# Hymba layer: gates of three second halves in pieces, meta rows in 34 columns, activation tiles by group

## The chip, the cores and the metric

The kernel runs on one core of a Trainium2 chip. Its engines are TensorE (PE, with its weight loads PEld), VectorE (DVE), ScalarE (ACT), GpSimd (POOL) and SyncE (SP), which issues the transfers. Each engine takes its instructions in a fixed order; a wait of one instruction holds all that stand behind it on the same engine. The metric is the device time of one launch in microseconds, as a median over runs.

## The reference

One decoder layer: 16 meta tokens are put ahead of 1024 tokens, a projection of 1024 to 3584 features feeds four heads of differential attention and four heads of HGRN2, an output projection follows, and a feed-forward part with a causal convolution of width 3 between its 1024 to 5632 and 2816 to 1024 products. The meta tokens are dropped at the end. In the feed-forward part the gate half of the 5632 features goes through the convolution and gelu and is multiplied with the up half. All in float32.

```python
def reference(x, meta_tokens, rel_bias_table, hgrn_lb_logits, ln_mix_pre, ln_mix_post,
              w_in, diff_lambda, diff_subln, hgrn_gnorm, w_out, ln_ffn_pre, ln_ffn_post,
              w_ffn_up, ffn_conv_w, ffn_conv_b, w_ffn_down):
...
    h = jnp.concatenate([meta, x], axis=1)
...
        a = rmsnorm(h, ln_mix_pre[l])
        proj = a @ w_in[l]
        dq, dk, dv, hq, hf, hi, hg = jnp.split(proj, SPLITS, axis=-1)
...
        y_diff = diff_attention(dq, dk, dv, diff_lambda[l], diff_subln[l], rel_bias_table, lam_init)
        y_hgrn = hgrn2(hq, hf, hi, hg, lb_all[l], hgrn_gnorm[l])
        mix = jnp.concatenate([y_diff, y_hgrn], axis=-1) @ w_out[l]
        h = h + rmsnorm(mix, ln_mix_post[l])
        a = rmsnorm(h, ln_ffn_pre[l])
        y = conv_ffn(a, w_ffn_up[l], ffn_conv_w[l], ffn_conv_b[l], w_ffn_down[l])
        h = h + rmsnorm(y, ln_ffn_post[l])
    return h[:, N_META:, :]

def conv_ffn(a, w_up, conv_w, conv_b, w_down):
    u = a @ w_up
    u = lax.conv_general_dilated(
...
        feature_group_count=C) + conv_b
    gate, up = jnp.split(u, 2, axis=-1)
    return (jax.nn.gelu(gate, approximate=True) * up) @ w_down
```

## The kernel before

**Numbers.** Every float32 operand of a product is split into a high part and a rest (hi, lo), and a product is three matmuls: hi by hi, hi by lo, lo by hi. Weights are split on ACT (hi) and on DVE or POOL (lo).

**Tokens.** 1040 tokens stand in nine blocks: block 0 are the 16 meta tokens, 1 to 8 have 128 tokens each. GROUPS puts blocks 0 to 2, 3 to 5 and 6 to 8 together: 272, 384 and 384 tokens. The projection (`proj_group`, `proj_step`, lines 219 to 239) goes over a group for each feature tile of 128: eight blocks k of the contraction, three matmuls each, with `ahi` and `alo` (the normalised activations, one tile each of 8 x 1040 floats a partition) as the streamed operand. `pre_hi` and `pre_lo` (lines 275 to 279) fill them from the transposed input.

**Output projection.** It has two halves of 512 columns. `out_first` does the first half while HGRN's last head still runs, with seven of the eight k blocks; the result goes to y0, and the eighth follows in `out_last` as soon as the head is there. Only the last two meta tokens are needed later (the convolution reaches two tokens back), so block 0 has two rows: `m0` holds hi and lo of 2 rows, `out_meta` (line 977) does three matmuls of 2 x 512 for each k through `out_part` (lines 966 to 975). Each `py` and `pz` takes a bank of PSUM by the name ip, of which there are two, so the third tile in line waits until the first has been read. In the second half the loop over blocks (order 1, 2, 0, 3 to 8) takes block 0 through the same `out_part` in four pieces of two k, and `post_a` (post norm and residual) follows each block. The blocks' split operands come back from DRAM as `mp` tiles.

**Feed-forward, up.** The 5632 features are 22 tiles ft of 128 gate and 128 up features. Tiles 0 and 1 are plain products (`plain_unit`). Tiles 2 to 21 are done in `unit` (lines 1322 to 1365): seven products j = 0 to 6 of half size for each half p of the tokens, in place of eight. A product is 12 matmuls of 256 or 258 columns. PE goes j by j and, within j, over p = 0, 1. Products 0 and 4 go to bank pa, 1, 3 and 5 to pb, 2 and 6 to pc. DVE combines them: `u2` behind j=1, `u3` and a part of `uu` behind j=3, the rest of `uu` behind j=5, a part of `ug` behind j=6; ACT copies pa. A bank is written again by PE only after such a combination has read it: j=3 of half p needs `u2` of that half done.

**The gate.** `gated` (line 1288) does the convolution of `ug` (gate) and `uu` (up): for each side ACT makes a shifted and scaled copy c (`conv`, line 1278) and DVE adds two taps to it (SCALAR_TENSOR_TENSOR, c0 for gate and c1 for up); ACT does gelu, POOL multiplies, SP stores to `gsc`. Four taps of 128 x 512 a half, eight a tile.

**Weights.** `prep(q)` makes the split weight q = 7 ft + j one tile ahead: POOL sums raw tiles `ra` to `ws`, ACT rounds to `uh`, DVE or POOL takes the rest to `ul`. It is called at the start of each j of the tile before.

**What sets the order.** The order within an engine comes out of the order of the code, of priorities and of waits that a scheduler plans; `behind(name)` holds instructions back behind a marked one (`u2`, `u3`, `x1`, `shift`). In tile 2 of before, the gate of tile 1's second half, which waits in `waiting`, is done behind `u3`, with four preps; all other gates follow their own half at once.

## Time and profile before

| | us |
|---|---|
| median of 3 runs (1326.83 to 1329.81) | 1327.34 |
| the profiled execution | 1325.77 |
| its span | 1324.0 |
| input projection, attention, HGRN (0 to 530) | 530 |
| output projection, first half (530 to 593) | 63 |
| output projection, second half (593 to 652) | 59 |
| up, plain tiles 0 and 1 (652 to 701) | 49 |
| up, tiles 2 to 21 (701 to 1104) | 403 |
| down (1104 to 1324) | 220 |

The profile's page gives busy time by engine over the whole span. The stages are read from the timeline, and a window of a stage gives the busy time of each engine in it. A row of the timeline has its start, its length, engine, line, operation and operands; in brackets stands how long the engine was idle ahead of it, and what ended that. A row with xN stands for N such instructions in a run.

### The profile page before, as it was taken

What the parts mean: (1) busy time and instruction counts of PE and PEld (TensorE: products, weight loads), DVE (VectorE), ACT (ScalarE), POOL (GpSimd) and SP (SyncE); (2) the same over time, 40 slices, a digit from 0 to 9 for tenths busy, and PEclk for the clock granted to TensorE, in tenths of its full rate; (3) what the DMA queues carried; (4) which work ended last, traced back from release to release, by engine and by line L of the source; (5) the groups of instructions that cost most, each with busy time, mean ns of one, the idle gap of its engine ahead of it and who ended that gap; (6) DMA issues with size and microseconds to landing.
All of it is one profiled execution on the core that took longest, in us unless ns stands there. A gap on an engine that the chain in (4) does not pass through costs nothing.

```text
span 1324.0 us, 26317 instructions
## 1 busy us (share of the span) xinstructions
PE 1276.6 (96%) x10227; PEld 1181.8 (89%) x10227; DVE 912.8 (69%) x1589; ACT 689.4 (52%) x1670; POOL 413.5 (31%) x324
## 2 busy tenths in 40 slices
PE   6999999999999999999999799999999999999997
PEld 5898899989999999777899799999999998888886
DVE  7666557564756465834778777877787876697587
ACT  7465346535654565545665454554454454554454
POOL 3211211121202120112147567667667641010021
PEclk9999999999999999999999899999999999999999
DMA  6331323132311011835713222222222324964363
GB/s 217 109 127 61 101 94 132 56 129 77 124 44 35 33 33 46 262 114 182 242 41 112 84 84 76 92 80 82 81 89 76 105 85 166 343 222 156 107 207 120
DMA packets 84371, 153.07 MB, mean 116 GB/s; under 512 B 9571, under 2 KB 19843, under 8 KB 84246
## 3 DMA queue, kind: packets, MB, share of 16 engines
q1 hardware_dynamic: 84246, 151.39, 34.0%
q8 instruction: 80, 1.31, 0.4%
q14 instruction: 45, 0.37, 0.1%
HBM read 112.69 MB, written 38.67 MB: 114 GB/s over the span
## 4 chain that ended last, share of the span: by engine, by line
PE 71%; DVE 6%; DMA 3%; ACT 3%; issue 2%; POOL 1%; SPq 1%; DVEq 0%; ACTq 0%; POOLq 0%
PE pd L1534 5%; PE pd L1535 5%; PE pd L1533 5%; PE pb L1336 4%; PE pb L1337 4%; PE pb L1338 4%; PE pa L1337 2%; PE pa L1336 2%; PE pa L1338 2%; PE pa L709 2%; PE pc L1338 2%; PE pc L1337 2%; PE pc L1336 2%; PE py L970 2%; PE py L974 2%
## 5 line engine op out<-in xcount | busy, mean ns | idle before, releaser
L1336 PE MATMUL pb<-t,uh 128*128 128x258 f32 (+1 forms) x480 | 135.4, 282 | 10.7 <-DVE u L54 10.7
L1337 PE MATMUL pb<-t,uh 128*128 128x258 f32 (+1 forms) x480 | 135.1, 281 | 0.0
L1338 PE MATMUL pb<-t,ul 128*128 128x258 f32 (+1 forms) x480 | 134.9, 281 | 0.0
L1534 PE MATMUL pd<-wl,gh 128*128 128x512 f32 (+1 forms) x314 | 121.4, 386 | 0.5 <-DVE wl L54 0.5
L1535 PE MATMUL pd<-wh,gl 128*128 128x512 f32 (+1 forms) x314 | 120.6, 384 | 0.0
L1533 PE MATMUL pd<-wh,gh 128*128 128x512 f32 (+1 forms) x314 | 120.1, 383 | 0.0
L54 DVE SCALAR_TENSOR_TENSOR c<-uu,cwt,c 128x512 f32<-128x512 f32 x88 | 92.4, 1050 | 22.5 <-ACT c L54 21.9
L1291 POOL TENSOR_TENSOR c<-c,c 128x512 f32<-128x512 f32 x44 | 68.4, 1554 | 124.1 <-ACT c L54 118.1
L1336 PEld LDWEIGHTS pb<-t,uh 128*128 128x128 f32 x480 | 91.5, 191 | 11.3 <-DVE u L54 11.3
L1337 PEld LDWEIGHTS pb<-t,uh 128*128 128x128 f32 x480 | 91.6, 191 | 0.0
L1338 PEld LDWEIGHTS pb<-t,ul 128*128 128x128 f32 x480 | 91.4, 190 | 0.0
L1337 PE MATMUL pa<-t,uh 128*128 128x258 f32 (+1 forms) x320 | 89.8, 281 | 0.0
L1338 PE MATMUL pa<-t,ul 128*128 128x258 f32 (+1 forms) x320 | 89.7, 280 | 0.0
L1336 PE MATMUL pa<-t,uh 128*128 128x258 f32 (+1 forms) x320 | 89.7, 280 | 0.0
L54 DVE SCALAR_TENSOR_TENSOR c<-ug,cwt,c 128x512 f32<-128x512 f32 x88 | 87.6, 996 | 1.7 <-ACT c L54 1.1
L1338 PE MATMUL pc<-t,ul 128*128 128x256 f32 x320 | 88.3, 276 | 0.0
L1336 PE MATMUL pc<-t,uh 128*128 128x256 f32 x320 | 88.3, 276 | 0.0
L1337 PE MATMUL pc<-t,uh 128*128 128x256 f32 x320 | 88.3, 276 | 0.0
L1534 PEld LDWEIGHTS pd<-wl,gh 128*128 128x128 f32 x314 | 59.0, 188 | 13.6 <-DVE wl L54 1.6
L1533 PEld LDWEIGHTS pd<-wh,gh 128*128 128x128 f32 x314 | 58.9, 188 | 12.6
L1535 PEld LDWEIGHTS pd<-wh,gl 128*128 128x128 f32 x314 | 59.0, 188 | 11.5
L54 ACT ACTIVATE pb<-S,ast 128x528 f32<-128x528 f32 (+7 forms) x72 | 46.5, 647 | 39.1 <-DVE ast L54 38.9
(411 smaller groups left out, 4210.3 us busy)
## 6 DMA issues: line engine op xcount, KB each, us to landing
ra<-in_wup_dram SPq DMA_DIRECT2D x80, 256.0 KB, 2.7
wd<-in_wdown_dram SPq DMA_DIRECT2D x44, 256.0 KB, 4.2
tsc<-wd SPq DMA_DIRECT2D x44, 256.0 KB, 2.7
gsc<-c SPq DMA_DIRECT2D x44, 256.0 KB, 2.0
wi<-tsc SPq DMA_DIRECT2D x44, 256.0 KB, 2.8
gi<-gsc SPq DMA_DIRECT2D x33, 256.0 KB, 3.7
wi<-in_wdown_dram SPq DMA_DIRECT2D x33, 256.0 KB, 3.0
msc<-mm SPq DMA_DIRECT2D x21, 256.0 KB, 3.5
```

The source lines that it names most:

```text
L54: ins = call(*args, **kw)
L709: T.matmul(po[:, :P], w_, vn[:, j], start=(j == 0), stop=(j == i))
L970: T.matmul(py[:r], mh[:, j, :r], hi, start=(first and j == 0), stop=False)
L974: T.matmul(py[:r], ml[:, j, :r], hi, start=False, stop=(last and k == k1 - 1))
L1291: G.tensor_tensor(cg, cg, cu, op=ALU.mult)
L1336: T.matmul(pt, hi[:, s], th[:, k], start=(first and k == 0), stop=False, skip_group_check=True)
L1337: T.matmul(pt, hi[:, s], tl[:, k], start=False, stop=False, skip_group_check=True)
L1338: T.matmul(pt, lo[:, s], th[:, k], start=False, stop=(k == 3), skip_group_check=True)
L1533: T.matmul(py, gh[:, s], wh, start=(k == 0 and pr not in (3, 7)), stop=False, skip_group_check=True)
L1534: T.matmul(py, gh[:, s], wl, start=False, stop=False, skip_group_check=True)
L1535: T.matmul(py, gl[:, s], wh, start=False, stop=(k == NH - 1), skip_group_check=True)
```

## The change

Three parts.

- The activation tiles `ahi` and `alo` become three tiles each, one for each group of blocks, with 272, 384 and 384 floats for each k. 32 floats of padding go ahead of them and 32 into the pool behind. What is computed and in which order stays.
- The two meta rows lie in a tile of 36 columns, hi in columns 0 and 1, lo in 32 and 33, zeros between. `out_meta` multiplies the 34 columns with the weights' hi and then lo: two matmuls for each k. Rows 0 and 1 and rows 32 and 33 of the result are then added: in the first half by an ACT copy and a DVE add into y0, in the second by an ACT copy to `low` and a DVE add in PSUM. The lo by lo product is now in the sum as well. `out_last` and block 1 stay as they were.
- The gates of the second halves (p = 1) of tiles 1, 2 and 3 wait for the next tile, and are done there in pieces: ACT's shifts at j=1 behind `u2` and `x1`, the taps of the up side behind `u3` of half 0, those of the gate side, gelu, product and store after j=3. Preps that would stand at j = 1 and 3 (in tile 2 at all of j = 0 to 3) come behind these pieces. From tile 4 on each gate follows its half at once.

```diff
@@ -180,5 +180,13 @@
     at_cm, atp = pool("at", 1)
-    ahi = atp.tile([P, KD, L], F32R, tag="ahi", name="ahi")
-    alo = atp.tile([P, KD, L], F32R, tag="alo", name="alo")
+    line_up(atp, 32)
+    acts = [[atp.tile([P, KD, start(b1 - 1) + P - start(b0)], F32R, tag=f"a{l}{g}", name=f"a{l}{g}") for g, (b0, b1) in enumerate(GROUPS)]
+            for l in ("hi", "lo")]
+
+    def act(l, ks, t0, t1):
+        g = 0 if t1 <= start(3) else 1 if t1 <= start(6) else 2
+        base = start(GROUPS[g][0])
+        return acts[l][g][:, ks, t0 - base:t1 - base]
+
     ws_cm, wsp = pool("wdsums", 5)
+    wsp.tile([P, 32], F32, tag="lineup_ws", name="lineup_ws", bufs=1)
 
@@ -231,7 +239,7 @@
         s = slice(P * (k % 4), P * (k % 4 + 1))
-        T.matmul(pt, hi[:, s], ahi[:, k, t0:t1], start=(k == 0), stop=False)
+        T.matmul(pt, hi[:, s], act(0, k, t0, t1), start=(k == 0), stop=False)
         yield cost
-        T.matmul(pt, hi[:, s], alo[:, k, t0:t1], start=False, stop=False)
+        T.matmul(pt, hi[:, s], act(1, k, t0, t1), start=False, stop=False)
         yield cost
-        T.matmul(pt, lo[:, s], ahi[:, k, t0:t1], start=False, stop=(k == KD - 1))
+        T.matmul(pt, lo[:, s], act(0, k, t0, t1), start=False, stop=(k == KD - 1))
         if k == KD - 1:
@@ -275,6 +283,6 @@
     def pre_hi(pv, ks, s):
-        return A.copy(ahi[:, ks, s], pv)
+        return A.copy(act(0, ks, s.start, s.stop), pv)
 
     def pre_lo(pv, ks, s):
-        return V.tensor_tensor(alo[:, ks, s], pv, ahi[:, ks, s].bitcast(F32), op=ALU.subtract)
+        return V.tensor_tensor(act(1, ks, s.start, s.stop), pv, act(0, ks, s.start, s.stop).bitcast(F32), op=ALU.subtract)
 
@@ -910,3 +918,4 @@
     y0 = yp.tile([P, NBLK, 512], F32, tag="y0", name="y0")
-    m0 = yp.tile([P, 2, KD, 2], F32R, tag="m0", name="m0")
+    m0 = yp.tile([P, KD, 36], F32R, tag="m0", name="m0")
+    G.memset(m0.bitcast(F32), 0.0)
     ssy = yp.tile([P, NBLK, 4], F32, tag="ssy", name="ssy")
@@ -947,4 +956,3 @@
         if i < 2:
-            m = (m0, kept)[i]
-            hi, lo = m[:, 0, k0:k1], m[:, 1, k0:k1]
+            hi, lo = (kept[:, 0, k0:k1], kept[:, 1, k0:k1]) if i else (m0[:, k0:k1, 0:2], m0[:, k0:k1, 32:34])
         elif k1 - k0 == 1:
@@ -976,4 +984,7 @@
 
-    def out_meta(py, wo, nk):
-        return out_part((m0[:, 0], m0[:, 1], 0, nk, 2), py, wo, True, True)
+    def out_meta(py, wo, k0, k1, last):
+        for k in range(k0, k1):
+            for l in range(2):
+                T.matmul(py[:34], m0[:, k, :34], wo[k][l], start=(k == 0 and l == 0), stop=(k == last and l == 1))
+                yield 216
 
@@ -1036,4 +1047,5 @@
         py = ps_in("py0_0")
-        yield from out_meta(py, wo0, 7)
-        A.copy(y0[:2, 0], py[:2])
+        yield from out_meta(py, wo0, 0, 7, 6)
+        A.copy(y0[:2, 0], py[32:34])
+        V.tensor_tensor(y0[:2, 0], y0[:2, 0], py[:2], op=ALU.add)
         while 0 not in finished:
@@ -1222,4 +1234,3 @@
         if i < 2:
-            m = (m0, kept)[i]
-            todo = [(m[:, 0, a:a + 2], m[:, 1, a:a + 2], a, a + 2, tok(i)[0]) for a in range(0, KD, 2)]
+            todo = [(kept[:, 0, a:a + 2], kept[:, 1, a:a + 2], a, a + 2, P) for a in range(0, KD, 2)]
         else:
@@ -1238,3 +1249,3 @@
                 trans(order[n - 2])
-            for _ in out_part(part, py, wo, c == 0, part is todo[-1]):
+            for _ in out_part(part, py, wo, c == 0, part is todo[-1]) if i else out_meta(py, wo, 2 * c, 2 * c + 2, KD - 1):
                 pass
@@ -1255,2 +1266,6 @@
             prep_plain(1, ("12", "22"))
+        if i == 0:
+            low = qp.tile([P, 512], F32, tag="tmp", name="low", bufs=1)
+            A.copy(low[:2], py[32:34])
+            V.tensor_tensor(py[:2], py[:2], low[:2], op=ALU.add)
         post_a(i, py)
@@ -1277,3 +1292,3 @@
 
-    def conv(ft, p, side, u):
+    def shift(ft, p, side, u):
         m = ft + NF * side
@@ -1282,10 +1297,10 @@
         marks["shift"] = A.activation(c, u[:, 2:2 + w], AF.Identity, bias=cbt[:, m:m + 1], scale=cwt[:, m, 2:3])
-        V.scalar_tensor_tensor(c, u[:, 1:1 + w], cwt[:, m, 1:2], c, ALU.mult, ALU.add)
-        V.scalar_tensor_tensor(c, u[:, 0:w], cwt[:, m, 0:1], c, ALU.mult, ALU.add)
         return c
 
-    def gated(ft, p, ug, uu, cu=None):
-        cg = conv(ft, p, 0, ug)
-        A.activation(cg, cg, AF.Gelu_apprx_tanh)
-        cu = cu or conv(ft, p, 1, uu)
+    def taps(ft, side, u, c):
+        m = ft + NF * side
+        for o in (1, 0):
+            V.scalar_tensor_tensor(c, u[:, o:o + 2 * HALF], cwt[:, m, o:o + 1], c, ALU.mult, ALU.add)
+
+    def gate(ft, p, cg, cu):
         G.tensor_tensor(cg, cg, cu, op=ALU.mult)
@@ -1295,3 +1310,12 @@
 
+    def gated(ft, p, ug, uu):
+        cg = shift(ft, p, 0, ug)
+        taps(ft, 0, ug, cg)
+        A.activation(cg, cg, AF.Gelu_apprx_tanh)
+        cu = shift(ft, p, 1, uu)
+        taps(ft, 1, uu, cu)
+        gate(ft, p, cg, cu)
+
     waiting = []
+    LATE = 4
 
@@ -1316,3 +1340,3 @@
         if ft and p:
-            waiting.extend(us)
+            waiting.append((ft, p, *us))
         else:
@@ -1363,3 +1387,6 @@
         seam(p, (ug, uu))
-        gated(ft, p, ug, uu)
+        if p and ft < LATE:
+            waiting.append((ft, p, ug, uu))
+        else:
+            gated(ft, p, ug, uu)
         yield
@@ -1424,3 +1451,4 @@
         for j in range(7):
-            if j > 3 or ft > 2:
+            late = bool(waiting)
+            if not late or j > 3 or (ft > 2 and j in (0, 2)):
                 prep(7 * (ft + 1) + j)
@@ -1428,10 +1456,19 @@
                 next(u)
-                if (ft, j, p) == (2, 3, 0):
-                    with behind("u3", "x1"):
-                        cu = conv(1, 1, 1, waiting[1])
-            if (ft, j) == (2, 3):
+                if late and (j, p) == (3, 0):
+                    with behind("u3"):
+                        taps(f, 1, uu, cu)
+            if late and j == 1:
+                f, q, ug, uu = waiting[0]
+                with behind("u2", "x1"):
+                    cu, cg = shift(f, q, 1, uu), shift(f, q, 0, ug)
+                with behind("u2", "shift"):
+                    prep(7 * (ft + 1) + (ft > 2))
+            if late and j == 3:
                 with behind("u3", "shift"):
-                    for q in range(4):
-                        prep(21 + q)
-                    gated(1, 1, *waiting, cu)
+                    taps(f, 0, ug, cg)
+                    A.activation(cg, cg, AF.Gelu_apprx_tanh)
+                    gate(f, q, cg, cu)
+                    for i in (3,) if ft > 2 else (1, 2, 3):
+                        prep(7 * (ft + 1) + i)
+                waiting.pop(0)
         if ft == NF - 3:
```

What DVE has in its queue from the end of tile 2 to `u2` of tile 3, before. (Names: tile and half stand behind c0, c1, u2, uu, ug; ul is a weight's lo part.)

```order
L54 SCALAR_TENSOR_TENSOR c1_2_0_8623<-uu2_0_8379,cwt_88,c1_2_0_8623 128x512
L54 SCALAR_TENSOR_TENSOR c1_2_1_8649<-uu2_1_8398,cwt_88,c1_2_1_8649 128x512
L54 SCALAR_TENSOR_TENSOR c0_2_0_8618<-ug2_0_8378,cwt_88,c0_2_0_8618 128x512
L54 SCALAR_TENSOR_TENSOR c1_2_0_8623<-uu2_0_8379,cwt_88,c1_2_0_8623 128x512
L54 SCALAR_TENSOR_TENSOR c0_2_0_8618<-ug2_0_8378,cwt_88,c0_2_0_8618 128x512
L54 TENSOR_TENSOR ug2_1_8397<-pc2_1_8457,u2_2_1_8400 128x256
L54 SCALAR_TENSOR_TENSOR c1_2_1_8649<-uu2_1_8398,cwt_88,c1_2_1_8649 128x512
L54 TENSOR_TENSOR ul28_8656<-ra4_11_8657,uh28_8655 128x512
L54 SCALAR_TENSOR_TENSOR c0_2_1_8644<-ug2_1_8397,cwt_88,c0_2_1_8644 128x512
L54 TENSOR_TENSOR ul29_8708<-ws2_8709,uh29_8707 128x512
L54 SCALAR_TENSOR_TENSOR c0_2_1_8644<-ug2_1_8397,cwt_88,c0_2_1_8644 128x512
L54 TENSOR_TENSOR u2_3_0_8672<-pb3_0_8713,x1_3_0_8671 128x256
```

And in the changed kernel, from the same point:

```order
L54 SCALAR_TENSOR_TENSOR c1_2_0_8619<-uu2_0_8375,cwt_88,c1_2_0_8619 128x512 x2
L54 TENSOR_TENSOR ug2_0_8374<-pc2_0_8458,u2_2_0_8377 128x256
L54 TENSOR_TENSOR ug2_1_8393<-pc2_1_8471,u2_2_1_8396 128x256
L54 SCALAR_TENSOR_TENSOR c0_2_0_8614<-ug2_0_8374,cwt_88,c0_2_0_8614 128x512
L54 TENSOR_TENSOR ul28_8641<-ra4_11_8642,uh28_8640 128x512
L54 SCALAR_TENSOR_TENSOR c0_2_0_8614<-ug2_0_8374,cwt_88,c0_2_0_8614 128x512
L54 TENSOR_TENSOR u2_3_0_8657<-pb3_0_8692,x1_3_0_8656 128x256
L54 TENSOR_TENSOR u2_3_1_8676<-pb3_1_8706,x1_3_1_8675 128x256
```

The four taps of c0_2_1 and c1_2_1 are gone from this stretch, and the split ul29 stands behind `u2`.

DVE in tile 4, from `u3` of half 0 to the last combination of `uu`, before:

```order
L54 TENSOR_TENSOR u3_4_0_8939<-pb4_0_8979,x1_4_0_8937 128x256
L54 TENSOR_TENSOR uu4_0_8936<-pc4_0_9011,u3_4_0_8939 128x256
L54 TENSOR_TENSOR u3_4_1_8958<-pb4_1_8993,x1_4_1_8956 128x256
L54 TENSOR_TENSOR uu4_1_8955<-pc4_1_9024,u3_4_1_8958 128x256
L54 TENSOR_TENSOR ul40_9102<-ra5_22_8925,uh40_9101 128x512
L54 TENSOR_TENSOR uu4_0_8936<-pb4_0_8979,x1_4_0_8937 128x258
```

And in the changed kernel:

```order
L54 TENSOR_TENSOR u3_4_0_8924<-pb4_0_8958,x1_4_0_8922 128x256
L54 SCALAR_TENSOR_TENSOR c1_3_1_8986<-uu3_1_8674,cwt_88,c1_3_1_8986 128x512
L54 TENSOR_TENSOR uu4_0_8921<-pc4_0_9000,u3_4_0_8924 128x256
L54 SCALAR_TENSOR_TENSOR c1_3_1_8986<-uu3_1_8674,cwt_88,c1_3_1_8986 128x512
L54 TENSOR_TENSOR u3_4_1_8943<-pb4_1_8972,x1_4_1_8941 128x256
L54 SCALAR_TENSOR_TENSOR c0_3_1_8988<-ug3_1_8673,cwt_88,c0_3_1_8988 128x512
L54 TENSOR_TENSOR uu4_1_8940<-pc4_1_9013,u3_4_1_8943 128x256
L54 SCALAR_TENSOR_TENSOR c0_3_1_8988<-ug3_1_8673,cwt_88,c0_3_1_8988 128x512
L54 TENSOR_TENSOR ul38_9062<-ws3_9063,uh38_9061 128x512
L54 TENSOR_TENSOR ul40_9098<-ra5_22_8910,uh40_9097 128x512
L54 TENSOR_TENSOR uu4_0_8921<-pb4_0_8958,x1_4_0_8922 128x258
```

Four taps of tile 3's second half and the split ul38 now stand in this stretch; behind it both kernels go on in the same order.

PE in the first half's meta block, the last k of py0_0 and what follows, before:

```order
L970 MATMUL py0_0_7079<-woh0_6_6374,m0_6300 2x512
L972 MATMUL py0_0_7079<-wol0_6_6375,m0_6300 2x512
L974 MATMUL py0_0_7079<-woh0_6_6374,m0_6300 2x512
L970 MATMUL pz0_7114<-woh0_7_6380,m0_6300 2x512
L972 MATMUL pz0_7114<-wol0_7_6381,m0_6300 2x512
L974 MATMUL pz0_7114<-woh0_7_6380,m0_6300 2x512
L970 MATMUL pz1_7123<-woh0_7_6380,kept_6323 128x512
```

And in the changed kernel:

```order
L988 MATMUL py0_0_7086<-woh0_6_6381,m0_6306 34x512
L988 MATMUL py0_0_7086<-wol0_6_6382,m0_6306 34x512
L978 MATMUL pz0_7115<-woh0_7_6387,m0_6306 2x512
L980 MATMUL pz0_7115<-wol0_7_6388,m0_6306 2x512
L982 MATMUL pz0_7115<-woh0_7_6387,m0_6306 2x512
L978 MATMUL pz1_7124<-woh0_7_6387,kept_6330 128x512
```

Three rows of 2 x 512 for a k have become two of 34 x 512; the products of the eighth k (pz0) stay three.

## The prediction

> **What bounds the kernel now.** I read the page first, for the engine that is never done early.

> ```profile
> span 1324.0 us, 26317 instructions
> PE 1276.6 (96%) x10227; PEld 1181.8 (89%) x10227; DVE 912.8 (69%) x1589; ACT 689.4 (52%) x1670; POOL 413.5 (31%) x324
> ```

> TensorE (PE) is busy for 1276.6 of 1324.0 us. So an edit is worth something in two ways only: it takes matmul time away, or it takes away part of the 47 us in which PE stands. The table of PE's waits says where it stands; I quote the largest wait and the one that the output projection has (columns: total us, times, longest).

> ```profile
> PE pb L1336 <- DVE u L54: 10.7, 3, 8.2
> PE py L970 <- DMA mp<-msc: 0.6, 2, 0.4
> ```

> One single wait of 8.2 us is the largest in the kernel. Windows over the up projection (span, PE, PEld, DVE, ACT, POOL busy with counts, PE clock, DMA share, GB/s) show that it is no steady state:

> ```profile
> 700.00:720.00 20.00, 20.00 (x174) 19.99 (x173) 18.35 (x19) 12.32 (x25) 14.72 (x9) 1.00 0.41 129
> 720.00:740.00 20.00, 11.80 (x92) 11.61 (x91) 15.85 (x20) 8.30 (x16) 13.48 (x10) 0.80 0.30 98
> 780.00:800.00 20.00, 20.00 (x175) 20.00 (x175) 15.72 (x23) 9.79 (x19) 13.49 (x10) 1.00 0.25 82
> ```

> Around 790 us PE never waits, with VectorE (DVE) at 15.72 of 20 us. At 700 to 720, in feature tile 2, DVE has 18.35 of 20 and falls behind; in the next window PE loses 8.2 us. PE's own timeline at this place (start, length, instruction, idle before it):

> ```profile
> 728.96 0.28 PE L1338 MATMUL pc<-t,ul 128*128 128x256 f32 x1
> 737.44 0.58 PE L1336 MATMUL pb<-t,uh 128*128 128x256 f32 x1 [8.20 <-DVE u L54]
> 742.30 0.35 PE L1337 MATMUL pb<-t,uh 128*128 128x256 f32 x1
> ```

> This is tile 3, product j=3 of half 0: it reuses bank pb, which `u2` has to read first. The stall costs more than 8.2 us. From 737.44 to 742.30 PE starts 22 matmuls in 4.86 us; at the 175 in 20 us of the undisturbed window they take 2.5. The clock column of two windows says why:

> ```profile
> 732.00:733.00 1.00, 0.00 (x0) 0.00 (x0) 1.00 (x3) 1.00 (x4) 0.81 (x1) 0.60 0.00 0
> 738.00:739.00 1.00, 1.00 (x7) 1.00 (x6) 0.74 (x1) 0.22 (x1) 1.00 (x1) 0.50 0.13 47
> ```

> The granted clock falls to half about 3 us into the stall (0.60 is the mean from 732 to 733), and stays there until 742.3. So this stall is worth 8.2 + 2.3 = **10.5 us**, if nothing takes its place.

> **Late gates, what goes at tile 3.** DVE's timeline from the end of tile 2 to the late `u2` (rows of shifted taps are those with c):

> ```profile
> 722.23 0.74 DVE L54 TENSOR_TENSOR uu<-pb,x 128x258 f32<-128x258 f32 x2
> 727.51 0.92 DVE L54 SCALAR_TENSOR_TENSOR c<-uu,cwt,c 128x512 f32<-128x512 f32 x1 [2.03 <-ACT c L54]
> 732.97 1.75 DVE L54 SCALAR_TENSOR_TENSOR c<-ug,cwt,c 128x512 f32<-128x512 f32 x1
> 734.64 1.74 DVE L54 TENSOR_TENSOR ul<-ws,uh 128x512 fp32r<-128x512 f32 x1
> 736.31 0.74 DVE L54 SCALAR_TENSOR_TENSOR c<-ug,cwt,c 128x512 f32<-128x512 f32 x1
> 736.97 0.74 DVE L54 TENSOR_TENSOR u<-pb,x 128x256 f32<-128x256 f32 x2
> ```

> From `uu` to `u2` DVE needs 14.7 us, and PE wanted `u2` at 729.24. By the order of instructions the rows at 727.51, 732.97, 736.31 and one at 731.71 are the four taps of c_2_1, the half that the change defers, and the split at 734.64 moves behind `u2`. By their starts the three quoted taps take 0.85, 1.67 and 0.66, the fourth 0.66, the split 1.67, and the wait for ACT ahead of the first goes with it, 2.03: 7.5 us together. `u2` would start at 729.4 and end at 729.8, so some 0.5 us of the stall stays (0 to 2). Tile 4 is built alike, and has nothing like the three a2 transforms that stood in DVE's queue during tile 2, so I put nothing there.

> ```profile
> 701.66 5.70 DVE L54 TENSOR_TENSOR t<-at,t 128x1024 fp32r<-128x1024 f32 x3
> ```

> **Late gates, what is late next.** The deferred taps have to run somewhere. In tiles 2, 3 and 4 they stand between `u3` and the last combinations `uu`, and tile 4 defers nothing: in tile 5 both c_4_0 and c_4_1 stand ahead of `u2` again, in the order that an undisturbed tile has. So tile 5 is the one to price. An undisturbed tile (4 to 5 of the kernel before):

> ```profile
> 761.79 0.41 DVE L54 TENSOR_TENSOR u<-pb,x 128x256 f32<-128x256 f32 x1
> 765.62 0.70 DVE L54 TENSOR_TENSOR ul<-ra,uh 128x512 fp32r<-128x512 f32 x1 [2.17 <-ACT uh L54]
> 766.52 0.43 DVE L54 TENSOR_TENSOR uu<-pb,x 128x258 f32<-128x258 f32 x1 [0.21 <-PE pb L1338]
> 778.03 0.74 DVE L54 TENSOR_TENSOR u<-pb,x 128x256 f32<-128x256 f32 x2
> ```

> Here `u3` is at 761.79, `uu` at 766.52, `u2` 11.5 us behind it. Between `u3` and `uu` DVE stands 2.17 + 0.21 = 2.4 us. PE needs bank pb again nine groups of 12 matmuls after `uu`'s group, 9 x 12 x 20/175 = 12.3 us, at 778.8; the first `u2` ends at 778.4, so the margin is another 0.4. The slack is **2.8 us**. Into this stretch the change puts, in tile 4, four taps and one split more (c_3_1's taps; `ul40` beside `ul38`). What one tap costs has two ends in the rows:

> ```profile
> 719.27 1.77 DVE L54 SCALAR_TENSOR_TENSOR c<-ug,cwt,c 128x512 f32<-128x512 f32 x1
> 721.57 0.74 DVE L54 SCALAR_TENSOR_TENSOR c<-ug,cwt,c 128x512 f32<-128x512 f32 x1
> ```

> The first runs beside a GpSimd (POOL) instruction, the second with POOL idle; start to start they cost 1.70 and 0.66. Splits have the same ends (1.67 and 0.60). So five instructions cost 3.2 to 8.5 us, and 0.4 to 5.7 of it is beyond the slack. I take 4.1: taps of 1.5 and a split of 0.9, near the upper end, since POOL's queue at this part of a tile is close to full:

> ```profile
> 722.26 1.30 POOL L1170 TENSOR_TENSOR ws<-ra,ra 128x512 f32<-128x512 f32 x1 [1.77 <-DMA ra<-in_wup_dram]
> 727.96 1.61 POOL L1170 TENSOR_TENSOR ws<-ra,ra 128x512 f32<-128x512 f32 x1
> ```

> five instructions between 722.26 and 729.57. A stall of 4.1 us is longer than the 3 us after which the clock fell above, so I add the same 2.3: 6.4 us in tile 5. The other parts move without a price: ACT's two shifts at j=1 go to an engine with 9.79 of 20 us busy, POOL's product and the store of the gate move later by a third of a tile and are read only by the down projection, 350 us on. Preps that wait behind `u3` hand their weights over one tile ahead. FFN together: -10.5 + 0.5 + 6.4 = **-3.6 us**, with -10.5 and +0.5 as ends.

> [...]

> **Meta rows.** 15 matmuls fewer (45 to 30), each with 512 columns. The groups by shape, and two starts of PE in the meta block's run:

> ```profile
> L970 PE MATMUL py<-woh,m 128*2 128x512 f32 x11 | 4.4, 402 | 0.0
> L970 PE MATMUL py<-woh,kept 128*128 128x512 f32 x11 | 4.3, 390 | 0.0
> ```

> ```profile
> 587.30 0.39 PE L972 MATMUL py<-wol,m 128*2 128x512 f32 x1
> 590.31 0.40 PE L974 MATMUL py<-woh,m 128*2 128x512 f32 x1
> ```

> A matmul with 2 rows out takes as long as one with 128 (402 and 390 ns), so 34 cost what 2 do. From 587.30 to 590.31 are 13 starts, 0.232 us each: 15 x 0.232 = 3.5 us less. Against it stand two new joins of the halves. The first is behind py_0, whose bank the third matmul group needs:

> ```profile
> 590.75 0.58 ACT L54 COPY y<-py 2x512 f32<-2x512 f32 x1 [0.87 <-PE py L974]
> ```

> ```profile
> 591.38 0.50 PE L970 MATMUL pz<-woh,kept 128*128 128x512 f32 x1
> ```

> ```profile
> 591.51 0.68 DVE L54 TENSOR_TENSOR y<-y,pz 2x512 f32<-2x512 f32 x1 [3.48 <-PE pz L974]
> ```

> `pz<-woh,kept` starts 0.05 us after this copy ends; now a DVE add of 2x512 (0.68) stands behind the copy and ahead of it: +0.7. The second join is in block 0 of the second half; it delays that block's ending by a copy and an add (0.58 + 0.68), beside matmuls of the next blocks. There 8 of the 15 go, so PE comes 1.9 us sooner to blocks whose `mp` transfers it already waited for twice; 0 to 1.9 is given back, I take 0.7, near the 0.6 that it waits now. Meta together: -3.5 + 0.7 + 0.7 = **-2.1 us** (-3.5 to -0.9). The memset of m0 runs on POOL, ahead of a block that comes last in this stage; POOL (fifth engine of the row) has 7.20 of 63 us busy there, so it costs nothing:

> ```profile
> 530.00:593.00 63.00, 61.11 (x708) 46.65 (x707) 38.54 (x97) 30.62 (x82) 7.20 (x8) 1.00 0.58 179
> ```

> **Activation tiles.** No instruction is added, removed or moved in the projection; only the rows' places in SBUF and their stride change. What there is to gain is the gap between these rows and a matmul that streams without one:

> ```profile
> 207.06 0.34 PE L234 MATMUL pi_hf<-alo,wh_hf 128*128 128x384 f32 x1
> 207.76 0.33 PE L236 MATMUL pi_hf<-ahi,wl_hf 128*128 128x384 f32 x1
> ```

> ```profile
> 727.03 0.28 PE L1336 MATMUL pc<-t,uh 128*128 128x256 f32 x1
> ```

> Four steps in 0.70 us are 0.175 for 384 columns; from 727.03 to the row at 728.96 are 17 steps, 0.1135 for 256 columns, or 0.170 for 384. The projection has 1,344 matmuls of 384 columns: 1344 x 0.005 = 6.4 us at most. No row shows whether a place of the rows costs anything, so the term lies between -6.4 and, by the same size in the other direction for a worse place, +1.5; I take **-1.5**, nearer to no effect.

> [...]

> **The sum.** -3.6 - 2.1 - 1.5 = -7.2 against this execution's own 1325.77 us: 1318.6. The median of the runs before is 1327.34, 1.6 above the profiled one, so I expect **1320.1** as a median.

> **Rivals.**
> 1. The stall goes and no other comes. For it: POOL may be idle while the deferred taps run, and then tile 5 is 0.4 late, with no fall of the clock: FFN -10.5 + 0.5 + 0.4 = -9.6, in all -13.2, so 1314.1. Against it: POOL's full queue in the window quoted.
> 2. The stall moves whole. Tile 5 is as late as tile 3 was (8.2 + 2.3), because `uu` also waits for ACT's shift as at 727.51; and the new places of the rows give nothing. Then -10.5 + 10.5 + 0.5 - 2.1 = -1.6: 1325.7. This is also the case in which the first part doesn't do what it says. Against it: tile 4 has no a2 transforms.
> 3. Slower: the taps hold the banks in each late tile. From j=3 DVE has four combinations (0.34 each) and four taps (1.38 to 1.70 beside POOL) to do, 6.9 to 8.2 us, while PE brings four groups in 5.5; two splits follow. Where pb and pc give less than 2.5 us of slack, PE waits some 2.5 us in each of tiles 2, 3 and 4, 7.5 us, and tile 5 still pays 10.5: -10.5 + 7.5 + 10.5 - 2.1 = +5.4, so 1332.7. Against it: in tile 2 of before two of the four taps and four splits stood in this stretch, and PE had 20.00 of 20.00.

> **Chances.** My forecast 0.47, rival 1 0.20, rival 2 0.23, rival 3 0.10. A measurement of this kernel can tell about 0.2%, 2.7 us, from no change. Forecast and rival 1 are faster by more than that (0.67), rival 2 lies within (0.23), rival 3 is slower (0.10). The range reaches from 1313.0, which takes in most of rival 1, to 1327.0, over rival 2, and leaves out rival 3 and the far end of rival 1; the forecast alone has 1317 to 1324 (a stall in tile 5 from 1.5 to 5.7 with the clock's fall, rows from -3 to 0).

> **What would show it.** In PE's waits the 8.2 under `pb <- DVE u` gone at j=3 of tile 3, and a wait of 3 to 6 us at the same product of tile 5, with a clock below 1.00 for some 5 us behind it; at 3 us or less the clock term falls too. `py<-wo,m0` with 30 rows of some 0.4 us, `pz<-woh,kept` 0.7 us later behind its copy, and `mp` waits of up to 2 us. In the projection a start-to-start of 384 columns below 0.175. The prediction is wrong if PE waits in tiles 2 to 4 (rival 3), if tile 5 shows none (rival 1), or if the projection's steps change by more than 5 ns.

## The result, and the profile after

Over 13 runs each the kernel before has a median of 1325.89 us (1322.80 to 1329.81) and the changed one 1322.63 us (1320.36 to 1324.26). The ratio is 0.9973, with a 95% interval from 0.9961 to 0.9985: 3.6 us faster, 2.0 to 5.2. The profiled execution has a span of 1321.4 us against 1324.0. The forecast was 7.2 us.

The page's row of busy time, after:

```profile
PE 1273.0 (96%) x10212; PEld 1180.3 (89%) x10212; DVE 920.0 (70%) x1591; ACT 689.2 (52%) x1671; POOL 419.0 (32%) x325
```

PE has 15 matmuls less and 3.6 us less to do, and stands about as long as before (1321.4 - 1273.0 = 48 us, against 47). Its waits say that the single stall has become two (columns: total us, times, longest; the other two of the first row's four are in tiles 19 and 20, and the kernel before has them too):

```profile
PE pb L1360 <- DVE u L54: 10.3, 4, 4.2
PE py L978 <- DMA mp<-msc: 0.9, 2, 0.6
PE pz L978 <- DVE y L54: 0.7, 1, 0.7
```

PE's timeline has them at tile 3 and tile 5, both at j=3 of half 0, and nothing at tile 4:

```profile
729.60 0.38 PE L1360 MATMUL pb<-t,uh 128*128 128x256 f32 x1 [3.59 <-DVE u L54]
...
773.13 0.58 PE L1360 MATMUL pb<-t,uh 128*128 128x256 f32 x1 [4.21 <-DVE u L54]
```

Windows around the two (span, then busy PE, PEld, DVE, ACT, POOL, PE clock, DMA share, GB/s):

```profile
726.00:730.00 4.00, 0.41 (x4) 0.41 (x4) 3.54 (x3) 0.76 (x2) 2.63 (x3) 1.00 0.19 70
730.00:734.00 4.00, 4.00 (x36) 4.00 (x36) 2.33 (x4) 3.62 (x7) 2.55 (x2) 1.00 0.50 180
768.00:773.00 5.00, 0.92 (x9) 0.73 (x7) 4.96 (x9) 2.94 (x6) 1.67 (x2) 0.92 0.30 109
773.00:779.00 6.00, 5.87 (x27) 5.87 (x28) 2.45 (x6) 1.58 (x4) 5.76 (x5) 0.50 0.14 52
```

Behind the first stall the clock stays at 1.00; behind the second it is at 0.50 for six microseconds. Where the time went is read best from the starts of the first matmul of each stage in both traces. An undisturbed tile lasts 19.5 us; what a tile has beyond that is its stall and what the clock costs behind it.

| us | before | after | change |
|---|---|---|---|
| first matmul of the output projection | 529.3 | 528.1 | -1.3 |
| from there to the meta block's first matmul | 56.0 | 56.8 | +0.8 |
| from the meta block's first matmul to plain tile 0 | 69.1 | 66.3 | -2.8 |
| plain tile 0 to tile 3 | 66.3 | 66.3 | 0.0 |
| tile 3, beyond an undisturbed tile | 10.8 | 3.9 | -6.9 |
| tile 5, beyond an undisturbed tile | 0.0 | 7.2 | +7.2 |
| tile 19 to the end | 281.0 | 281.2 | +0.2 |

The rest, tile 6 to 19 among it, is the same to 0.1 us. In this pair of traces the gates give back at tile 5 what they save at tile 3, and the meta rows are most of what is gained. Part of that split is chance: in the traces stalls of 2.3 to 4.2 us cost from 0.3 to 3.1 us beyond their own length (last section).

The rows of VectorE (DVE) that answer to those of tile 2 to 3 before:

```profile
717.46 1.78 DVE L54 TENSOR_TENSOR ul<-ra,uh 128x512 fp32r<-128x512 f32 x1
719.15 0.75 DVE L54 TENSOR_TENSOR uu<-pb,x 128x258 f32<-128x258 f32 x2
720.46 2.45 DVE L54 SCALAR_TENSOR_TENSOR c<-uu,cwt,c 128x512 f32<-128x512 f32 x2 [0.55 <-ACT c L54]
722.83 0.74 DVE L54 TENSOR_TENSOR ug<-pc,u 128x256 f32<-128x256 f32 x2
724.18 1.69 DVE L54 SCALAR_TENSOR_TENSOR c<-ug,cwt,c 128x512 f32<-128x512 f32 x1 [0.60 <-ACT c L54]
725.79 1.75 DVE L54 TENSOR_TENSOR ul<-ra,uh 128x512 fp32r<-128x512 f32 x1
727.46 1.75 DVE L54 SCALAR_TENSOR_TENSOR c<-ug,cwt,c 128x512 f32<-128x512 f32 x1
729.13 0.41 DVE L54 TENSOR_TENSOR u<-pb,x 128x256 f32<-128x256 f32 x1
```

The order is the one foreseen, but from `uu` to `u2` it takes 10.0 us and not 7.2: the four taps and the split take 7.6 us together. GpSimd (POOL) in the same stretch:

```profile
720.72 1.64 POOL L1182 TENSOR_TENSOR ws<-ra,ra 128x512 f32<-128x512 f32 x1 [2.03 <-DMA ra<-in_wup_dram]
...
727.07 1.59 POOL L1182 TENSOR_TENSOR ws<-ra,ra 128x512 f32<-128x512 f32 x1
```

It has five instructions back to back from 720.72 to 728.66.

### The profile page after: what moved, and what is told of

Read it like the earlier page. It is cut to its first block, busy times and chain, and to the rows that moved or that the text cites. A ratio compares the mean times of both kernels' runs of the same rounds, so it can differ in the third digit from the quotient of the medians.

```text
span 1321.4 us, 26287 instructions
## 1 busy us (share of the span) xinstructions
PE 1273.0 (96%) x10212; PEld 1180.3 (89%) x10212; DVE 920.0 (70%) x1591; ACT 689.2 (52%) x1671; POOL 419.0 (32%) x325
## 4 chain that ended last, share of the span: by engine, by line
PE 64%; DVE 7%; issue 2%; ACT 2%; DMA 2%; SPq 0%; POOL 0%; DVEq 0%; ACTq 0%; POOLq 0%
PE pd L1571 5%; PE pd L1572 5%; PE pd L1570 5%; PE pb L1360 4%; PE pb L1361 4%; PE pb L1362 4%; PE pa L1361 2%; PE pa L1360 2%; PE pa L1362 2%; PE pc L1362 2%; PE pc L1360 2%; PE pc L1361 2%; DVE c L54 2%; PE py L978 2%; PE pa L717 2%
## 5 line engine op out<-in xcount | busy, mean ns | idle before, releaser
L54 DVE SCALAR_TENSOR_TENSOR c<-uu,cwt,c 128x512 f32<-128x512 f32 x88 | 96.5, 1097 | 19.8 <-ACT c L54 19.2
L54 DVE SCALAR_TENSOR_TENSOR c<-ug,cwt,c 128x512 f32<-128x512 f32 x88 | 89.8, 1020 | 2.9 <-ACT c L54 2.3
L1570 PEld LDWEIGHTS pd<-wh,gh 128*128 128x128 f32 x314 | 59.0, 188 | 11.5
L54 ACT ACTIVATE pb<-S,ast 128x528 f32<-128x528 f32 (+7 forms) x72 | 46.6, 648 | 39.2 <-DVE ast L54 39.1
```

The source lines that it names most:

```text
L54: ins = call(*args, **kw)
L1570: T.matmul(py, gh[:, s], wh, start=(k == 0 and pr not in (3, 7)), stop=False, skip_group_check=True)
```

## The experiments

Ratios are to the kernel before, over several runs each. Where a time stands in place of a ratio, there is a single execution of that kernel. "Beyond" is a tile's time over 19.5 us, from the traces.

### The parts alone

`e1_gates` has the third part of the diff only (`shift`, `taps`, `gate`, `LATE` and the loop over tiles).

```diff
         seam(p, (ug, uu))
-        gated(ft, p, ug, uu)
+        if p and ft < LATE:
+            waiting.append((ft, p, ug, uu))
+        else:
+            gated(ft, p, ug, uu)
```

> Only the late gates, on the kernel before. Theory A (the gates give back at tile 5 what they save at tile 3): the wait of 8.2 us at tile 3 becomes 3 to 4 us with the clock at 1.00, a wait of 4 to 5 us comes at tile 5 with the clock at 0.50 for 5 to 6 us behind it, tile 2 to tile 6 together last as long as before within 1 us, and the ratio is 0.999 to 1.001. Theory B (the gates gain the 3.6 us that was forecast and something else lost it in the whole change): ratio 0.9965 to 0.998.

Ratio 0.9985 (0.9973 to 0.9997). Its longest wait for `u` is 2.9 us:

```profile
PE pb L1345 <- DVE u L54: 8.0, 4, 2.9
```

Tile 3 waits 2.6 and tile 5 2.9 us; beyond are 4.3 and 4.8, 9.1 together against 10.8 before. The clock fell behind both (0.50 from 734 to 736 and from 779 to 781). So the stall does move to tile 5, as theory A says, but both halves are smaller than in the whole change, and 1.6 us are left. The ratio fits between the two theories and settles neither by itself.

`e2_meta` has the second part only.

```diff
-        yield from out_meta(py, wo0, 7)
-        A.copy(y0[:2, 0], py[:2])
+        yield from out_meta(py, wo0, 0, 7, 6)
+        A.copy(y0[:2, 0], py[32:34])
+        V.tensor_tensor(y0[:2, 0], y0[:2, 0], py[:2], op=ALU.add)
```

> Only the meta rows in 34 columns, on the kernel before. Theory A (this part is most of the gain): 15 matmuls of 0.232 us go, 0.7 us comes back as a wait of pz for y, 0 to 1 as waits for mp; from the first meta matmul to the first plain tile 2.3 to 2.9 us less, nothing else moves, ratio 0.9975 to 0.9985. Theory B (it is hidden by waits for mp and for the joins): under 1 us less there, ratio above 0.9992.

Ratio 0.9988 (0.9977 to 0.9999). From the meta block to plain tile 0 it takes 66.4 us against 69.1, 2.7 less, and its waits are those of the whole change:

```profile
PE py L970 <- DMA mp<-msc: 0.9, 2, 0.5
PE pz L970 <- DVE y L54: 0.7, 1, 0.7
```

The nine kernels of this study with the meta part take 66.0 to 66.9 us there, the three without 67.9 to 69.1. The stretch is as theory A has it; the ratio lies just above its 0.9975 to 0.9985, and the interval holds both.

`e3_acts` has the first part only.

```diff
-    ahi = atp.tile([P, KD, L], F32R, tag="ahi", name="ahi")
-    alo = atp.tile([P, KD, L], F32R, tag="alo", name="alo")
+    line_up(atp, 32)
+    acts = [[atp.tile([P, KD, start(b1 - 1) + P - start(b0)], F32R, tag=f"a{l}{g}", name=f"a{l}{g}") for g, (b0, b1) in enumerate(GROUPS)]
+            for l in ("hi", "lo")]
```

> Only the activation tiles by group with their padding, on the kernel before. Theory A (the place of the rows costs a little): the step between matmuls of 384 columns goes from 174.9 to about 173.4 ns and the projection is 1 to 2 us shorter, ratio 0.9985 to 0.9995. Theory B (the place costs nothing): step 174.5 to 175.3, ratio 0.9995 to 1.0005.

Ratio 0.9993 (0.9982 to 1.0005): the times don't tell. The trace does: the mean step of some 955 pairs of matmuls of 384 columns that follow each other in one accumulation is 174.9 ns before, 175.0 in `e1_gates` and `e2_meta`, and 173.2 here. In all nine kernels with this part it is between 173.2 and 173.4. Two rows of the changed kernel, three steps apart:

```profile
206.33 0.33 PE L244 MATMUL pi_hf<-ahi,wl_hf 128*128 128x384 f32 x1
...
206.84 0.34 PE L244 MATMUL pi_hf<-ahi,wl_hf 128*128 128x384 f32 x1
```

These three steps, 0.51 us, are among the quicker ones at 0.170 each; the mean is what counts. Which of the rows' place, their stride or the padding does it, no run separates. 1,344 matmuls at 1.6 ns are 2.2 us. How much of it reaches the end of the projection is less sure: its first matmul of the output projection stands at 528.1 to 532.0 us in the nine kernels with the part (mean 529.4) and at 529.3 to 532.2 in the three without (mean 530.5), a scatter larger than the difference.

### What ends at tile 5

`e4_late21` and `e5_late5` change the number of deferred tiles.

```diff
-    LATE = 4
+    LATE = 21
```

> The changed kernel with the second halves deferred in all tiles up to 20 instead of 3. Theory A (the stall in tile 5 is the price of ending the deferral, and a deferred tile is sustainable): tile 5's wait of 4.2 us and its 3.0 us of half clock go, no wait above 1 us comes from tile 4 to tile 18, some 7 us less than the changed kernel, ratio to before about 0.992. Theory B (a deferred tile is not sustainable: its taps run at 1.45 us beside GpSimd, so VectorE falls behind a little in each): waits of 2 to 5 us in several of tiles 5 to 20, ratio to before 0.999 or more.

Ratio 0.9959 (0.9943 to 0.9975). Tiles 4 to 18 wait for nothing, tile 3 2.7 us. Its waits:

```profile
PE pb L1360 <- DVE u L54: 6.0, 2, 3.3
```

The other of the two, 3.3 us, is in tile 19, where DVE has splits of the down projection ahead of `u3` as well; the stretch from tile 19 to the end is 2.1 us longer than before, which takes back part of tile 5's 7.2. So a deferred tile is sustainable (theory A), and the gain is smaller than the 7 us expected; its interval overlaps the changed kernel's (0.9961 to 0.9985), so the times alone don't set the two apart.

`e5_late5` has LATE = 5.

> The changed kernel with one tile more deferred (tiles 1 to 4). Theory A (the stall belongs to the first tile after the last deferred one, and more deferred tiles neither build it up nor wear it down): no wait at tile 5, one of 3.5 to 4.9 us at j=3, half 0 of tile 6; tile 2 to tile 7 lasts as long as in the changed kernel within 1 us if the clock falls behind it as well. Theory C (slack of 4 us a tile wears the delay down): tile 6 waits under 2 us.

A single execution, 1321.49 us. Tile 5 waits for nothing, and tile 6 does:

```profile
792.72 0.38 PE L1360 MATMUL pb<-t,uh 128*128 128x256 f32 x1 [2.81 <-DVE u L54]
```

The stall moves with the end of the deferral. At 2.8 us it is smaller than the 3.5 to 4.9 expected by theory A and larger than the 2 of theory C. It is as large as in `e1_gates` (2.9) and 1.4 us smaller than in the changed kernel, both with one tile less. Up to tile 3 the changed kernel, `e4_late21` and `e5_late5` have the same code, and tile 3 waits 3.6, 2.7 and 2.6 us: executions differ by 1 us. Whether one more tile wears the stall down a little is therefore not shown.

`e6_taps_u2` runs the up side's two deferred taps behind `u2`.

```diff
-                if late and (j, p) == (3, 0):
-                    with behind("u3"):
-                        taps(f, 1, uu, cu)
...
                     cu, cg = shift(f, q, 1, uu), shift(f, q, 0, ug)
+                with behind("u2", "shift"):
+                    taps(f, 1, uu, cu)
```

> The changed kernel with the two taps of the up side of a deferred half run behind u2 instead of behind u3 of half 0, where VectorE idles 2.2 us in tile 4. Theory A (tile 5 is late because uu of tile 4 is late, by what the deferred taps add between u3 and uu beyond the idle time there): uu of tile 4 comes about 2 us sooner against its product, the wait at tile 5 falls from 4.2 to 2 to 3 us. Theory D (tile 5 is late by the load of its own eight taps, wherever tile 4's deferred ones ran): it stays at 3.8 to 4.5.

A single execution, 1319.21 us. The wait at tile 5 is 3.2 us, which lies between what the two theories expect. Against the first matmul of tile 5, `uu` of tile 4 comes 1.0 us ahead here and 0.1 in the changed kernel: it comes 0.9 us sooner and not 2, and the wait is 1.0 us shorter. The rows of the changed kernel, whose tile 5 starts at 760.39:

```profile
760.32 0.41 DVE L54 TENSOR_TENSOR uu<-pb,x 128x258 f32<-128x258 f32 x1
...
772.66 0.74 DVE L54 TENSOR_TENSOR u<-pb,x 128x256 f32<-128x256 f32 x2
```

From `uu` to `u2` it is 12.3 us in the stalled tile of `e1_gates`, the changed kernel, `e5_late5` and `e6_taps_u2`, and the lead of `uu` and the wait add up to 4.3 us in each: 1.38 and 2.89, 0.07 and 4.21, 1.47 and 2.81, 1.04 and 3.23. So the delay of `uu` goes into the stall one to one, as theory A says. That this edit made `uu` sooner is not shown by it: `e1_gates` and `e5_late5` have a larger lead with the taps in their old place. There the clock fell behind tile 3, where the stall cost 1.7 and 1.9 us beyond its own length; of the two kernels in which it did not, this one has the larger lead, by half of what theory A expected.

### What sets the length of the queue

`e7_prep0` has LATE = 21, and the split of j=0 behind `u2` in deferred tiles.

```diff
-            if not late or j > 3 or (ft > 2 and j in (0, 2)):
+            if not late or j > 3 or (ft > 2 and j == 2):
...
-                    prep(7 * (ft + 1) + (ft > 2))
+                    for i in (0, 1) if ft > 2 else (0,):
+                        prep(7 * (ft + 1) + i)
```

> Second halves deferred to tile 20, and in deferred tiles the split of j=0 (ul28 in tile 3) behind u2 instead of ahead of it: one VectorE split less in the stretch from uu of tile 2 to u2 of tile 3. Theory A (the wait left at tile 3 is the length of that queue, each instruction at 1.7 us beside GpSimd): tile 3's wait falls by 1.5 to 1.9 us from the 2.7 of the kernel with tile 20, to about 1. Theory E (what ends last there is GpSimd or ScalarE, not VectorE's queue): under 0.5 us less. Ratio to before 0.993 to 0.996 by A.

Ratio 0.9966 (0.9953 to 0.9979). Tile 3 waits 2.9 us: theory A of this run falls. DVE's rows of the stretch:

```profile
722.10 0.74 DVE L54 TENSOR_TENSOR uu<-pb,x 128x258 f32<-128x258 f32 x2
723.40 3.51 DVE L54 SCALAR_TENSOR_TENSOR c<-uu,cwt,c 128x512 f32<-128x512 f32 x2 [0.55 <-ACT c L54]
726.83 0.74 DVE L54 TENSOR_TENSOR ug<-pc,u 128x256 f32<-128x256 f32 x2
728.18 3.34 DVE L54 SCALAR_TENSOR_TENSOR c<-ug,cwt,c 128x512 f32<-128x512 f32 x2 [0.60 <-ACT c L54]
731.44 0.41 DVE L54 TENSOR_TENSOR u<-pb,x 128x256 f32<-128x256 f32 x1
```

One split less, and the four taps take 6.85 us where they took 5.4 in `e4_late21` (2.96, 1.68 and 0.74): from `uu` to `u2` it is 9.3 us against 9.5. So the taps take 1.45 us longer, most of the 1.74 that the split took there. That points at POOL, and `e9_no_sums` tests it.

`e9_no_sums` leaves POOL's weight sums out and DVE's order as it is in the changed kernel.

```diff
-        G.tensor_tensor(sums[nm], a, b, op=op)
+        if sparse[0]:
+            A.copy(sums[nm], a)
+        else:
+            G.tensor_tensor(sums[nm], a, b, op=op)
...
+        sparse[0] = ft in (4, 5, 6)
```

> The changed kernel, where GpSimd's sums of raw weights for tiles 4, 5 and 6 (done during tiles 3 to 5) are left out: ScalarE copies one of the two raw tiles in place of each sum, so those tiles' products are not the reference's. VectorE's instructions and their order are those of the changed kernel. Theory F (taps and splits take 1.4 to 1.75 us because GpSimd's instructions shut them out, and that sets both waits): the rows between uu of tile 2 and u2 of tile 3, and between u3 of tile 4 and u2 of tile 5, fall towards 0.7 us each; tile 3's wait falls from 2.6 to 3.6 to under 1.2, tile 5's from 4.2 to under 1.5. Theory G (VectorE's queue of that many instructions and ScalarE's shifts set them): both waits stay within 0.7 us of the changed kernel's.

A single execution, 1315.65 us. The same DVE rows of tile 2 to 3:

```profile
718.66 1.77 DVE L54 TENSOR_TENSOR ul<-ra,uh 128x512 fp32r<-128x512 f32 x1
720.36 0.74 DVE L54 TENSOR_TENSOR uu<-pb,x 128x258 f32<-128x258 f32 x2
...
725.38 0.75 DVE L54 SCALAR_TENSOR_TENSOR c<-ug,cwt,c 128x512 f32<-128x512 f32 x1 [0.61 <-ACT c L54]
726.04 0.68 DVE L54 TENSOR_TENSOR ul<-ra,uh 128x512 fp32r<-128x512 f32 x1
726.64 0.74 DVE L54 SCALAR_TENSOR_TENSOR c<-ug,cwt,c 128x512 f32<-128x512 f32 x1
727.31 0.42 DVE L54 TENSOR_TENSOR u<-pb,x 128x256 f32<-128x256 f32 x1
```

The last tap, split and tap go from 1.69, 1.75 and 1.75 to 0.75, 0.68 and 0.74, and `uu` to `u2` from 10.0 to 6.95 us, close to the 7.2 of the prediction. Tile 5's wait falls from 4.2 to 0.7 us, as theory F expects. Tile 3 still waits 1.7 us, more than the 1.2 that it gave as a bound. POOL's work ahead of `uu` was left: a sum for tile 3, a split and a gate's product from 714.87 to 719.89, and the split at 718.66 runs beside the product. `uu` comes 2.8 us behind tile 3's first matmul here and 1.7 in the changed kernel, which takes back 1.1 of the 3.0 us. Beyond are 2.3 and 1.0 us, and the clock stays at 1.00 behind both. Each wait is shorter than in any of the other kernels that have it with this order (2.6 to 3.6 and 2.8 to 4.2), one execution though it is. So both waits hang on what DVE's taps and splits take beside POOL (1.69 to 1.75 us here, against 0.68 to 0.75 without POOL's sums), far more than on how many instructions DVE has.

### Kernels that beat both

`e8_both` joins the edits of `e6_taps_u2` and `e7_prep0` with LATE = 21; `e10_taps21` has the one of `e6_taps_u2` with LATE = 21.

> Both: second halves deferred to tile 20, the up side's taps and the split of j=0 behind u2. Theory A: tile 3 waits about 1 us or less, no tile from 4 to 18 waits over 1 us, tile 19 waits for the down projection's first splits, 3 to 4 us, as with the kernel with tile 20; ratio to before 0.992 to 0.996. Theory D (the queue of a deferred tile is only rearranged): tile 3 as before this edit, 2.7 to 3.6 us, ratio 0.996 or more.

> Second halves deferred to tile 20 and the up side's taps behind u2, the split of j=0 back ahead of u2 (e8_both without its prep edit). If the prep edit is what costs small waits in deferred tiles and gives nothing at tile 3, this is as fast as e8_both or up to 1 us faster: tile 3 waits 2.5 to 3.6 us, tiles 4 to 18 nothing, ratio to before 0.991 to 0.995. If the prep edit is what helps at tile 19, this is slower, 0.994 to 0.997.

`e8_both`: 0.9922 (0.9903 to 0.9942). Tile 3 waits 2.3 us, more than the 1 of theory A; tiles 4 to 18 nothing; and tile 19 to the end is 279.5 us, 1.5 less than before, where a wait of 3 to 4 us was expected. In its waits nothing of that size is left at tile 19; the longest of the four is tile 3's, and the other three, in tiles 2 and 19, are 1.1 us together:

```profile
PE pb L1360 <- DVE u L54: 3.4, 4, 2.3
```

`e10_taps21`: 0.9943 (0.9928 to 0.9958). Tile 3 waits 2.8 us, tiles 4 to 18 nothing, tile 19 2.1 us, and tile 19 to the end is 281.8 us. The times put it behind `e8_both`, but the intervals overlap, and in the traces its span is shorter (1313.5 against 1315.3), so which of the two is faster stays open. Both are faster than the changed kernel's 0.9973 and, by their intervals, than each timed kernel without the whole deferral. `e8_both` is also clear of `e7_prep0` (0.9953 to 0.9979), from which it differs only by the place of the up side's taps.

## Why the prediction was right, and where it was off

**Direction and range held; the size was half.** 3.6 us came in place of 7.2. The range was wide enough to take in rival 2 (1325.7) as well, and the measured 1322.6 lies about halfway between that and the forecast's 1320.1, so the time alone doesn't favour the forecast's mechanism. Its own signs are mixed: the wait at tile 5 came, but the one at tile 3 did not go, and by its last line a wait in tiles 2 to 4 speaks against it. By its terms:

- *What goes at tile 3*, "some 0.5 us of the stall stays (0 to 2)": this is the step that failed. 3.6 us stayed in the profiled execution, and 2.3 to 3.6 in all kernels with the gates, `e9_no_sums` aside. The instructions that go were the right ones; those that stay were priced as they stood in the trace of before, 4.9 us for four taps and a split (0.98, 1.77, 0.74, 0.74, 0.68). POOL was idle there from 729.57 to 732.20, beside two of the taps:

```profile
724.50 0.98 DVE L54 SCALAR_TENSOR_TENSOR c<-uu,cwt,c 128x512 f32<-128x512 f32 x1 [1.20 <-ACT c L54]
...
728.36 1.77 DVE L54 SCALAR_TENSOR_TENSOR c<-ug,cwt,c 128x512 f32<-128x512 f32 x1
730.05 0.74 DVE L54 SCALAR_TENSOR_TENSOR c<-uu,cwt,c 128x512 f32<-128x512 f32 x1
730.71 0.74 DVE L54 SCALAR_TENSOR_TENSOR c<-ug,cwt,c 128x512 f32<-128x512 f32 x1
...
732.37 0.68 DVE L54 TENSOR_TENSOR ul<-ra,uh 128x512 fp32r<-128x512 f32 x1
```

  In the new order nearly each runs beside POOL, and the five take 7.6 us. `e9_no_sums` shows it: without POOL's sums the stretch from `uu` to `u2` takes 6.95 us and not 10.0.
- *What is late next*: right in place and size. Tile 5 was named, at j=3 of half 0, with 4.1 us; it waits 4.2 (2.9 in `e1_gates`, 2.8 one tile later in `e5_late5`). The closeness is in part luck. The added instructions cost less than priced, four taps at 1.37 from start to start and a split at 0.60, 6.1 us in place of 6.9; `uu` comes 3.8 us later than in an undisturbed tile, and from `uu` to `u2` it takes 12.3 us in place of 11.5, which the sum had left out; less the margin of 0.4 that makes 4.2. The working was also inconsistent: at tile 5 the taps were priced at 1.5, near the upper end of 0.66 to 1.70, and at tile 3 most of the instructions at the lower end (0.68 to 0.74).
- *The clock*: "A stall of 4.1 us is longer than the 3 us after which the clock fell" gave 2.3; it cost 3.0 at tile 5 and next to nothing at tile 3, whose wait of 3.6 is longer than 3 us too. The 3 us as a bound are not borne out; the last section has what is.
- *FFN together* was -3.6; the traces have +0.3 for the whole change (-6.9 + 7.2) and -1.6 for `e1_gates`. Timed, the gates alone gave 0.15% (0.03 to 0.27), 2 us, more than the pair of traces shows.
- *Meta rows*: -2.1 forecast, -2.8 in the pair of traces, -2.7 in the trace of `e2_meta`; timed, 0.12% (0.01 to 0.23), 1.6 us. The 0.7 us behind the new join came as priced (the wait `pz <- y` is 0.7):

```profile
589.25 0.68 DVE L54 TENSOR_TENSOR y<-y,py 2x512 f32<-2x512 f32 x1 [1.69 <-ACT y L54]
```

```profile
589.98 0.50 PE L978 MATMUL pz<-woh,kept 128*128 128x512 f32 x1 [0.68 <-DVE y L54]
```

  The transfers gave back 0.3 and not 0.7. A matmul with 34 rows out takes what one with 2 took (401 and 402 ns):

```profile
L988 PE MATMUL py<-woh,m 128*34 128x512 f32 x11 | 4.4, 401 | 0.0
```

- *Activation tiles*: -1.5 forecast; the steps give 2.2 us at most, the times 0.9 us (0.9993) with an interval that holds 0. That the places of the rows do something is shown; that it reaches the end is not.

**Rivals.** The gates' part came out nearly as in rival 2 (it gives what it takes), by a smaller stall at each of two places and not by one moved whole; the meta part, which that rival has too, kept the total on the faster side, and what the rows add, which it had at nothing, isn't settled. Rival 1 is what `e9_no_sums` comes near to, and there POOL is idle, as the rival had it. Rival 3's waits in each deferred tile came in none of the runs with the change's own order; in `e7_prep0` tiles 4 to 6 have 0.2 to 0.8 us.

What POOL adds to an instruction of DVE stood in the trace of before (a tap took 1.77 us beside POOL and 0.74 with POOL idle), and the runs have the same two sizes: 1.69 to 1.75 for two taps and a split in the changed kernel, 0.68 to 0.75 for the same three in `e9_no_sums`, without POOL's sums. The price beside POOL should have been taken at tile 3 too.

## What to carry to other kernels

When an edit moves instructions of DVE, price what stays as well as what moves, and against POOL's queue at the new time: here one tap took 1.75 us beside POOL and 0.74 without its sums, and the stretch from `uu` to `u2`, with four taps and a split, 10.0 and 6.95. A deferral has an end, and the first stage after it takes both shares; look for the stall there, or let the deferral run to the end of the loop (0.9922 to 0.9966 in four such kernels here against 0.9973; only the two with the taps behind `u2` as well are faster beyond the intervals). Where a large stall is cut in two, look at the clock behind each part, in more than one execution, before counting the gain.

## What the runs showed of the hardware

The clock's fall isn't a matter of a stall's length alone. Behind 3.6 us (tile 3 of the changed kernel) it stayed at 1.00; behind 2.3 us in `e8_both` and 2.7 in `e4_late21` it fell to 0.50. What a stall of 2.3 to 4.2 us in tiles 3, 5 and 6 cost beyond its own length was 0.3 us in four cases, 0.9 in one (with a second, short wait), 1.7 to 1.9 in five and 3.0 to 3.1 in two.

```profile
727.62:731.04 3.42, 1.10 (x11) 0.91 (x9) 3.28 (x3) 0.41 (x1) 2.35 (x2) 1.00 0.07 28
731.04:734.45 3.41, 3.41 (x16) 3.41 (x17) 2.30 (x4) 3.41 (x8) 1.29 (x1) 0.50 0.46 154
```

PE is busy for 1.10 of 3.42 us, and the next step is at 0.50. The clock of the changed kernel did not change anywhere near tile 3; counted back from its fall at 772.23, the step's border cuts the stall of 3.6 us in two:

```profile
724.44:727.86 3.42, 1.56 (x14) 1.37 (x13) 3.42 (x3) 0.58 (x2) 3.34 (x3) 1.00 0.46 153
727.86:731.27 3.41, 1.68 (x14) 1.68 (x15) 2.10 (x3) 2.03 (x4) 2.10 (x2) 1.00 0.41 141
```

PE is busy for 1.56 and 1.68 us, and the clock stays. Over tiles 2 to 21 of all twelve traces PE stood for 0.56 to 1.00 of the step ahead of each of the twelve falls, and for at most 0.55 of any step at full clock behind which the clock stayed. Worked out from these numbers, as an estimate: a step of 3.41 us at 0.50 costs up to half of itself, 1.7 us, and less where it begins within the stall (the two cases of 3.0 to 3.1 us had two such steps); and in this kernel a stall below 1.9 us (0.56 of 3.41) would not lower the clock, one above 3.8 (twice that) would, and between them it would depend on where the stall falls on the grid. The changed kernel, `e4_late21` and `e5_late5` are the same program up to tile 3, and there this cost was 0.3, 3.1 and 1.9 us: one execution's profile doesn't price it.
